# Row normalisation ahead of the transposes, copy evictions on ScalarE, and a later transpose of the residual, in a hybrid decoder layer on one core

## The chip, the cores and the metric

One NeuronCore of a Trainium2 chip runs the whole layer as one program. The metric is the device time of one execution in microseconds (us). Engine names: PE = TensorE matmul, PEld = TensorE weight load, DVE = VectorE, ACT = ScalarE, POOL = GpSimd, SP = SyncE, whose queue issues nearly all DMAs.

## The reference

Two groups of rows share one set of weights: 1024 prompt rows and 32 sample rows (8 sequences of 4), each of 1024 numbers.

```python
h = RMSNorm(x) * norm_mix_w
p = h @ w_in     # 5640 columns: q|k|v (512 each), conv q|k|v (1536), z (512), a, b (4+4), gate_A, gate_B (1024 each)
# branch A: stick-breaking attention, 8 heads x 64, strictly causal
s = sigmoid(q.k/8 + bias[head]);  w[i,j] = s[i,j] * prod_{j<l<i} (1 - s[i,l]);  o_A = w @ v
# branch B: conv of width 4, SiLU, l2norm, gated delta rule over chunks, 4 heads x 128, then norm and silu(z)
x = x + (sigmoid(gate_A) * (o_A @ w_pa) + sigmoid(gate_B) * (o_B @ w_pb)) @ w_o
x = x + relu(RMSNorm(x) @ w_up)^2 @ w_down;   y = RMSNorm(x)
```

The sample rows attend to 256 cached positions through a page table and have their own conv and delta states. All is float32. k, v, the last conv rows and the final states are outputs too.

## The kernel before

Everything is kept transposed: features on the 128 partitions, the 1056 rows (tokens) along the free dimension. A float32 product is made of three matmuls on parts rounded to fp32r: hi x hi, hi x lo, lo x hi (`dense`, L124 to L129), where ACT writes hi as a rounded copy and DVE writes lo = value - hi.

**Start (L76 to L238).** Nine row tiles `xn` are loaded; then the weights of the first two projections (`load_w`, L109) are queued on SP between the stores of `xT_d`. Each raw tile is transposed by PE (`xtp`, 8 transposes of 128x128), DVE multiplies by the norm weight (`xw`, L217), ACT keeps a raw copy `xs` (L218), which is stored to DRAM as `xT_d` for the residual, and `xw` is split into `xh`, `xl`, four column chunks `CX` of 256, 256, 256 and 288 tokens. Beside it `token_sum` and `finish_r` work out each row's 1/rms: a Square with sum on ACT (L192), a power on POOL (L105), a diagonal times ones on PE (`prb`, L201). The result R holds it for every token on all partitions. So the normalisation is not in `xh`, `xl`; every eviction of a projection multiplies by R on DVE.

**Projections (`proj`, L240).** A job is 128 columns of `w_in`: per chunk 24 matmuls into a PSUM bank, then an eviction. With the argument f set the banks are `psf` (two), else `psd` (two). Jobs: four heads of branch B, k, q, v, z each (`conv_job` L344, `z_job` L365); q, k, v of attention in pairs of heads (L753; tiles `ft`, three slots in pool `fk`); 16 gate jobs (`pd_g`, L978 to L990), whose result goes through a Sigmoid in place (L988) and to DRAM `gA_d`, `gB_d`.

**Attention (L886 to L975).** `attn_load` brings q and k of one head from DRAM onto both partition halves and splits them (L900 to L904). `weights` then works for each block of 128 queries: scores `sc` on PE, Sigmoid on ACT, mask and 1 - s on POOL (L917, L920), a backward product scan on DVE (L924), the product s x scan (L925), transposes `wt` on PE, copies on ACT, and `po` on PE, copied to `oT` by DVE (L954). Heads 0 to 5 go one after another, heads 6 and 7 together (`attn_last`).

**Order.** The source order is the priority. A planner runs through a modelled timeline and gives each engine the ready instruction of highest priority, so later jobs fill gaps of earlier ones: attention's q, k, v and the gates run inside branch B's chain and the cached attention, and the product with `w_pb` (`pb`, L1045 to L1056) runs beside attention. On the chip each engine then works through its list in that fixed order, SP's queue too. Memory is a stack: `xh`, `xl` and `fk` lie in pools closed by `xctx.close()` (L993), and the tiles of `pb` (`tb`, `obh`, `obl`) are laid over them; each waits until the tile under it is free.

After attention come `pa` with `w_pa` and the merge, `w_o` with the residual read from `xT_d` (L1159), and the channel mixer.

## Time and profile before

| | |
|---|---|
| runs shown | 1778.04, 1778.16, 1778.8 us; median 1778.16 |
| profiled execution | 1763.56 us, span 1761.9 us, clock 0.995 |
| instructions | 34413 |
| DMA | 224.91 MB, 39.4% of 16 engines on the main queue |

The span is the time from the first to the last recorded instruction. A row of "windows" gives, for a stretch of it, how long each engine was busy, in the order PE, PEld, DVE, ACT, POOL, with instruction counts, then the granted TensorE clock, the DMA share and GB/s. A row of "lines" groups the instructions of one source line: busy time and mean ns of one, then the idle time ahead of them with what ended it. In a timeline the first number is the start, the second the length, and brackets hold the idle time before.

### The profile page before, as it was taken

To read this page: it belongs to the slowest core of one execution; us is meant where nothing else is said; L and a number is where in the kernel's file an instruction comes from. 1 tells how busy PE (TensorE), PEld (TensorE's weight loads), DVE (VectorE), ACT (ScalarE), POOL (GpSimd) and SP (SyncE) were. 2 spreads that over 40 slices of the span, in tenths; PEclk is the share of its full clock that TensorE was granted. 3 is DMA by queue.
4 is the path that set the end of the run, shared out by engine and by line. 5 is a ranking of instruction groups with operands and counts; after the bars stand their busy time and mean duration, and the time that the engine had idled before them with its cause. 6 is when DMAs were issued, how large, how long until landed. Compare 5 with 4: busy or idle time off the path is not lost.

```text
span 1761.9 us, 34413 instructions
## 1 busy us (share of the span) xinstructions
PE 1703.9 (97%) x13831; PEld 1642.1 (93%) x13831; DVE 1236.8 (70%) x2584; ACT 746.0 (42%) x1370; POOL 229.1 (13%) x251
## 2 busy tenths in 40 slices
PE   7999999999999999999979999999999999999998
PEld 6999999999999778878869999999999899999998
DVE  6768587787436424899878576887777768788854
ACT  6441324232323122654533455554444564444354
POOL 1022111020001061465450000000000000000000
PEclk9999999999999999999999999999999999999999
DMA  7332132133426275354204645554443683532321
GB/s 223 76 103 78 43 103 85 57 116 90 135 79 186 81 237 146 106 164 110 75 35 129 183 129 151 158 150 147 136 152 131 232 293 129 171 121 95 123 73 76
DMA packets 229532, 224.91 MB, mean 128 GB/s; under 512 B 22186, under 2 KB 191507, under 8 KB 229372
## 3 DMA queue, kind: packets, MB, share of 16 engines
q1 hardware_dynamic: 225062, 214.09, 39.4%
q0 software_dynamic: 2560, 8.39, 1.5%
q8 instruction: 109, 1.79, 0.4%
q10 hardware_dynamic: 1750, 0.23, 0.1%
q14 instruction: 51, 0.42, 0.1%
HBM read 153.63 MB, written 69.04 MB: 126 GB/s over the span
## 4 chain that ended last, share of the span: by engine, by line
PE 78%; DVE 8%; issue 5%; DMA 5%; ACT 2%; POOL 1%; SPq 1%; POOLq 0%; ACTq 0%; DVEq 0%
PE pu L129 6%; PE pu L127 6%; PE pu L128 6%; PE pw L128 5%; PE pw L127 5%; PE pw L129 5%; PE pd_g L127 3%; PE pd_g L129 3%; PE pd_g L128 3%; DVE s L925 1%; DVE pr L924 1%; PE px L128 1%; PE pv L127 1%; PE px L129 1%; PE px L127 1%
## 5 line engine op out<-in xcount | busy, mean ns | idle before, releaser
L129 PE MATMUL pu<-Xh,ul 128*128 128x264 f32 x812 | 230.7, 285 | 0.0
L127 PE MATMUL pu<-Xh,uh 128*128 128x264 f32 x812 | 229.8, 283 | 0.4 <-ACT uh L1137 0.4
L128 PE MATMUL pu<-Xl,uh 128*128 128x264 f32 x812 | 230.1, 284 | 0.0
L127 PE MATMUL pw<-hc,w 128*128 128x264 f32 x728 | 206.2, 285 | 4.3 <-ACT w L1384 4.3
L128 PE MATMUL pw<-hc,w 128*128 128x264 f32 x728 | 206.9, 286 | 0.0
L129 PE MATMUL pw<-hc,w 128*128 128x264 f32 x728 | 202.2, 284 | 0.0
L127 PEld LDWEIGHTS pu<-Xh,uh 128*128 128x128 f32 x812 | 153.0, 188 | 0.7 <-ACT uh L1137 0.6
L128 PEld LDWEIGHTS pu<-Xl,uh 128*128 128x128 f32 x812 | 152.5, 188 | 0.0
L129 PEld LDWEIGHTS pu<-Xh,ul 128*128 128x128 f32 x812 | 152.0, 188 | 0.0
L127 PE MATMUL pd_g<-xh,wh_g 128*128 128x256 f32 (+1 forms) x512 | 150.0, 293 | 1.2 <-DVE gt L985 1.2
L129 PE MATMUL pd_g<-xh,wl_g 128*128 128x256 f32 (+1 forms) x512 | 149.6, 292 | 0.0
L128 PE MATMUL pd_g<-xl,wh_g 128*128 128x256 f32 (+1 forms) x512 | 149.1, 291 | 0.0
L127 PEld LDWEIGHTS pw<-hc,w 128*128 128x128 f32 x728 | 137.4, 189 | 4.5 <-ACT w L1384 4.5
L128 PEld LDWEIGHTS pw<-hc,w 128*128 128x128 f32 x728 | 137.2, 189 | 0.0
L129 PEld LDWEIGHTS pw<-hc,w 128*128 128x128 f32 x728 | 136.0, 189 | 0.0
L127 PEld LDWEIGHTS pd_g<-xh,wh_g 128*128 128x128 f32 x512 | 98.2, 192 | 5.3 <-issue 3.3
L128 PEld LDWEIGHTS pd_g<-xl,wh_g 128*128 128x128 f32 x512 | 98.2, 192 | 4.2 <-issue 4.1
L129 PEld LDWEIGHTS pd_g<-xh,wl_g 128*128 128x128 f32 x512 | 98.2, 192 | 2.7 <-issue 2.4
L924 DVE TENSOR_TENSOR_SCAN pr<-am 128x127 f32<-128x127 f32 (+7 forms) x64 | 91.2, 1432 | 5.7 <-POOL am L920 5.5
L105 POOL TENSOR_TENSOR fr<-fr,powc 128x3 f32<-128x3 f32 x4 | 3.4, 858 | 680.8 <-DVE fr L1495 645.1
L1384 ACT ACTIVATE w<-a 128x512 fp32r<-128x512 f32 x78 | 43.3, 621 | 94.0 <-PE pw L129 86.6
L129 PE MATMUL px<-mh,wl_wo 128*128 128x264 f32 x256 | 72.6, 287 | 1.3 <-DVE wl_wo L1138 1.2
(588 smaller groups left out, 5267.8 us busy)
## 6 DMA issues: line engine op xcount, KB each, us to landing
hc_d<-t SPq DMA_DIRECT2D x26, 924.0 KB, 4.9
hc<-hc_d SPq DMA_DIRECT2D x91, 264.0 KB, 3.0
a<-in_w_down_dram SPq DMA_DIRECT2D x52, 256.0 KB, 5.5
ws_g<-in_w_in_dram SPq DMA_DIRECT2D x16, 512.0 KB, 5.2
ws_wo<-in_w_o_dram SPq DMA_DIRECT2D x32, 256.0 KB, 3.0
ua<-in_w_up_dram SPq DMA_DIRECT2D x16, 512.0 KB, 4.9
ub<-in_w_up_dram SPq DMA_DIRECT2D x16, 512.0 KB, 4.2
gA_d<-gt SPq DMA_DIRECT2D x8, 528.0 KB, 3.6
```

The source lines that it names most:

```text
L105: G.tensor_tensor(out, in_, powc[: out.shape[0], which:which + 1].to_broadcast([out.shape[0], n]), op=ALU.pow)
L127: PE.matmul(pt[:, :n], lhsT=wh[k], rhs=xh[k], start=(k == 0), stop=False)
L128: PE.matmul(pt[:, :n], lhsT=wh[k], rhs=xl[k], start=False, stop=False)
L129: PE.matmul(pt[:, :n], lhsT=wl[k], rhs=xh[k], start=False, stop=(k == nk - 1))
L924: V.tensor_tensor_scan(pr[:, n - 2::-1], am_r, am_r, 1.0, op0=ALU.mult, op1=ALU.bypass)
L925: V.tensor_tensor(s[:, :n], s[:, :n], pr[:, :n], op=ALU.mult)
L1384: S_.activation(tl[:, 0], src, AF.Copy)
```

## The change

Several edits in one:

- Row tiles are normalised before they are transposed: Square on ACT, power on POOL, then one DVE instruction multiplies by 1/rms and by the norm weight, which is broadcast to all partitions as `nmb`. PE transposes the result; ACT writes `xh` and DVE `xl` straight from PSUM. R, `token_sum`, `finish_r` and `xw` are gone.
- The weights of the first three projections are loaded among the row tiles; `xn` has seven slots instead of nine.
- Projections of branch B and the gates are evicted by ACT, as Copy or, for the gates, as Sigmoid.
- q and k of attention are split at their eviction (hi by ACT, lo by DVE) and stored as two tensors each; `attn_load` only loads. `ft` has four slots.
- The scan loses its memset and is read one column shifted; `oT` is copied by ACT.
- After the gates a new loop loads the nine raw row tiles again, transposes them through the `psf` banks, copies them by ACT and stores `xT_d`, with two `ft` slots a tile.
- The last gate no longer lives in R, and goes through DRAM like the others.

```diff
-    nrow = sp.tile([8, P], F32, name="nrow", bufs=1)
-    SY.dma_start(nrow, norm_mix_w.rearrange("o (k p) -> (o k) p", p=P))
+    nmb = sp.tile([P, D], F32, name="nmb", bufs=1)
...
-    xns = []
+    winv = w_in[0].rearrange("(k p) n -> p k n", p=P)
+    xns, w0s = [], []
     for t in range(9):
-        xn = sp.tile([P, D], F32, tag="xn", name=f"xn{t}", bufs=9)
+        xn = sp.tile([P, D], F32, tag="xn", name=f"xn{t}", bufs=7)
         n = P if t < 8 else NS
         SY.dma_start(xn[:n], x_prompt[0, t * P:(t + 1) * P, :] if t < 8 else x_sample.rearrange("s t d -> (s t) d"))
         xns.append(xn)
+        if t == 1:
+            SY.dma_start(nmb, norm_mix_w.to_broadcast([P, D]))
+        if t in (1, 3, 5):
+            wp = wpool if t == 1 else gw if t == 5 else sp
+            st = wp.tile([P, 8, P], F32, tag="wst", name=f"ws_u0{t}", bufs=1)
+            col = {1: 2048, 3: 1536, 5: 2560}[t]
+            SY.dma_start(st, winv[:, :, col:col + P])
+            w0s.append(st)
...
@@ -183,52 +188,29 @@
         xhc[c] = xp.tile([P, KT, CX[c][1]], F32R, name=f"xh{c}")
         xlc[c] = xp.tile([P, KT, CX[c][1]], F32R, name=f"xl{c}")
     fk = pool("fk", stack=xctx)
-    winv = w_in[0].rearrange("(k p) n -> p k n", p=P)
     w0 = []
-
-    def token_sum(t):
-        n = P if t < 8 else NS
-        junk = sp.tile([P, D], F32, tag="junk", name=f"junk{t}", bufs=1)
-        S_.activation(junk[:n], xns[t][:n], AF.Square, accum_out=sst_[:n, t:t + 1])
-        V.tensor_scalar(sst_[:n, t:t + 1], sst_[:n, t:t + 1], 1.0 / D, EPS, op0=ALU.mult, op1=ALU.add)
-
-    def finish_r(t):
-        n = P if t < 8 else NS
-        rpow(rstd[:n, t:t + 1], sst_[:n, t:t + 1], 0, 1)
-        dg = sp.tile([P, P], F32, tag="dg", name=f"dg{t}")
-        V.tensor_scalar(dg[:n, :n], ident[:n, :n], rstd[:n, t:t + 1], None, op0=ALU.mult)
-        prb = gtile(f"prb{t}")
-        PE.matmul(prb[:, :n], lhsT=ones[:n, :], rhs=dg[:n, :n], start=True, stop=True)
-        V.tensor_copy(R[:, t * P:t * P + n], prb[:, :n])
-
     for t in range(9):
         n = P if t < 8 else NS
         c0 = t * P
         xn = xns[t]
-        xw = sp.tile([P, KT, P], F32, tag="xw", name=f"xw{t}")
-        xs = sp.tile([P, KT, P], F32, tag="xs", name=f"xs{t}")
+        junk = sp.tile([P, D], F32, tag="junk", name=f"junk{t}", bufs=1)
+        S_.activation(junk[:n], xn[:n], AF.Square, accum_out=sst_[:n, t:t + 1])
+        V.tensor_scalar(sst_[:n, t:t + 1], sst_[:n, t:t + 1], 1.0 / D, EPS, op0=ALU.mult, op1=ALU.add)
+        rpow(rstd[:n, t:t + 1], sst_[:n, t:t + 1], 0, 1)
+        V.scalar_tensor_tensor(xn[:n], xn[:n], rstd[:n, t:t + 1], nmb[:n], op0=ALU.mult, op1=ALU.mult)
+        cc = min(t // 2, 3)
+        co = c0 - CX[cc][0]
         for hf in range(2):
-            pt = ttile(f"xtp{t}_{hf}")
+            pt = (ttile, gtile)[hf](f"xtp{t}_{hf}")
             pv = pt.rearrange("p (k c) -> p k c", k=4)
             for k in range(4):
                 kk = hf * 4 + k
                 tr(pv[:, k, :n], xn[:n, kk * P:(kk + 1) * P], n)
-            ks = slice(hf * 4, hf * 4 + 4)
-            V.tensor_tensor(xw[:, ks, :n], pv[:, :, :n], nmw[:, ks].unsqueeze(2).to_broadcast([P, 4, n]), op=ALU.mult)
-            S_.activation(xs[:, ks, :n], pv[:, :, :n], AF.Copy)
-        cc = min(t // 2, 3)
-        co = c0 - CX[cc][0]
-        S_.activation(xhc[cc][:, :, co:co + n], xw[:, :, :n], AF.Copy)
-        V.tensor_tensor(xlc[cc][:, :, co:co + n], xw[:, :, :n], xhc[cc][:, :, co:co + n].bitcast(F32), op=ALU.subtract)
-        SY.dma_start(xT_d[:, :, c0:c0 + n].rearrange("k p c -> p k c"), xs[:, :, :n])
-        if t in (1, 2):
-            col = 2048 if t == 1 else 1536
-            w0.append(load_w(winv[:, :, col:col + P], f"u0{t}"))
-        if t % 2 == 1 or t == 8:
-            for u in range(t - t % 2, t + 1):
-                token_sum(u)
-            for u in range(t - t % 2, t + 1):
-                finish_r(u)
+            xh_ = xhc[cc][:, hf * 4:hf * 4 + 4, co:co + n]
+            S_.activation(xh_, pv[:, :, :n], AF.Copy)
+            V.tensor_tensor(xlc[cc][:, hf * 4:hf * 4 + 4, co:co + n], pv[:, :, :n], xh_.bitcast(F32), op=ALU.subtract)
+        if t in (1, 3, 5):
+            w0.append(load_w(None, f"u0{t}", gw if t == 5 else wpool, w0s[t // 2]))
...
@@ -348,12 +327,11 @@

         def evac(c, o, n, pt):
             if c < 3:
-                V.tensor_tensor(up[:, 3 + o:3 + o + n], pt[:, :n], R[:, o:o + n], op=ALU.mult)
+                S_.activation(up[:, 3 + o:3 + o + n], pt[:, :n], AF.Copy)
                 return
             m = NP - o
-            V.tensor_tensor(up[:, 3 + o:3 + NP], pt[:, :m], R[:, o:NP], op=ALU.mult)
-            V.tensor_tensor(us[:, i, :, 3:7], pt[:, m:n].rearrange("p (s t) -> p s t", s=8),
-                            R[:, NP:T].rearrange("p (s t) -> p s t", s=8), op=ALU.mult)
+            S_.activation(up[:, 3 + o:3 + NP], pt[:, :m], AF.Copy)
+            V.tensor_copy(us[:, i, :, 3:7], pt[:, m:n].rearrange("p (s t) -> p s t", s=8))
             V.tensor_scalar(cv, up[:, 0:NP], cwv(0, i), None, op0=ALU.mult)
             for j in range(1, 4):
...
@@ -366,7 +344,7 @@
         z = zp.tile([P, T], F32, tag="zz", name=f"z{h}")

         def evac(c, o, n, pt):
-            V.tensor_tensor(z[:, o:o + n], pt[:, :n], R[:, o:o + n], op=ALU.mult)
+            S_.activation(z[:, o:o + n], pt[:, :n], AF.Copy)
             if c == 3:
                 S_.activation(z, z, AF.Silu)
                 G.tensor_copy(zs[:, h, :], z[:, NP:T])
@@ -392,9 +370,9 @@
     def gdn_head(h):
         (jk, kT), (jq, qT), (jv, vT) = conv_job(4 + h, f"k{h}"), conv_job(h, f"q{h}"), conv_job(8 + h, f"v{h}")
         if h == 0:
-            proj([jk, jq], ws=w0)
+            proj([jk, jq], ws=w0[0:2])
             decays()
-            proj([jv], f=True, wp=gw)
+            proj([jv], f=True, ws=w0[2:3])
...
@@ -747,28 +725,46 @@
     vk = pool("vk", stack=bctx, side="right")


+    NFT = 4
     sbb = cst.tile([P, NH], F32, name="sbb")
     nc.scalar.dma_start(sbb, sb_bias.to_broadcast([P, NH]))
     for p in range(4):
         for nm, col, keep_s in (("q", 0, qsT), ("k", 512, ksT), ("v", 1024, vsT)):
-            f = fk.tile([P, T], F32, tag="ft", name=f"{nm}f{p}", bufs=3)
-
-            def ev(c, o, n, pt, f=f):
+            hi = lo = f = None
+            if nm != "q":
+                f = fk.tile([P, T], F32, tag="ft", name=f"{nm}f{p}", bufs=NFT)
+            if nm != "v":
+                hi = fk.tile([P, NP], F32R, tag="ft", name=f"{nm}h{p}", bufs=NFT)
+            if nm == "q":
+                lo = fk.tile([P, NP], F32, tag="ft", name=f"{nm}l{p}", bufs=NFT)
+
+            def ev(c, o, n, pt, f=f, hi=hi, lo=lo, keep_s=keep_s[:, p, :]):
+                m = min(n, NP - o)
                 with tc.high_priority():
-                    V.tensor_tensor(f[:, o:o + n], pt[:, :n], R[:, o:o + n], op=ALU.mult)
+                    if hi is not None:
+                        S_.activation(hi[:, o:o + m], pt[:, :m], AF.Copy)
+                    if lo is not None:
+                        V.tensor_tensor(lo[:, o:o + m], pt[:, :m], hi[:, o:o + m].bitcast(F32), op=ALU.subtract)
+                    if f is not None:
+                        S_.activation(f[:, o:o + m], pt[:, :m], AF.Copy)
+                    if m < n:
+                        V.tensor_copy(keep_s, pt[:, m:n])

             proj([(col + p * P, f"a{nm}{p}", ev)], f=True)
-            G.tensor_copy(keep_s[:, p, :], f[:, NP:T])
-            if nm != "v":
-                SY.dma_start((q_d if nm == "q" else k_d)[p], f[:, 0:NP])
             if nm != "q":
-                nt = fk.tile([P, NP], F32, tag="ft", name=f"nt{nm}{p}", bufs=3)
+                nt = fk.tile([P, NP], F32, tag="ft", name=f"nt{nm}{p}", bufs=NFT)
                 for hf, pt in enumerate(tr8(f, f"n{nm}{p}", lambda n_: dtile(n_, True))):
                     S_.activation(nt[:, hf * 512:(hf + 1) * 512], pt, AF.Copy)
                 dst = nk_prompt if nm == "k" else nv_prompt
                 SY.dma_start(dst[0, 0, :, :, 2 * p:2 * p + 2, :].rearrange("c t h d -> t c (h d)"), c8(nt))
                 if nm == "v":
                     SY.dma_start(v_d[p], c8(nt))
+            if nm == "k":
+                lo = f[:, 0:NP]
+                V.tensor_tensor(lo, lo, hi.bitcast(F32), op=ALU.subtract)
+            if nm != "v":
+                for dst, src in zip(q_d if nm == "q" else k_d, (hi.bitcast(F32), lo)):
+                    SY.dma_start(dst[p], src)


...
@@ -890,18 +886,11 @@
         kh = ak.tile([P, NP], F32R, tag="kh", name=f"kh{hh}")
         kl = ak.tile([P, NP], F32R, tag="kl", name=f"kl{hh}")

-        def load2(src, name):
-            t_ = ak.tile([P, NP], F32, tag="qd", name=f"{name}{hh}", bufs=1)
-            for r in range(2):
-                SY.dma_start(t_[64 * r:64 * r + 64], src[p, rs])
-            return t_
-
-        qd = load2(q_d, "qd")
-        S_.activation(qs, qd, AF.Copy)
-        V.tensor_tensor(qs[64:128], qd[64:128], qs[64:128].bitcast(F32), op=ALU.subtract)
-        kd_ = load2(k_d, "kd")
-        S_.activation(kh, kd_, AF.Copy)
-        V.tensor_tensor(kl, kd_, kh.bitcast(F32), op=ALU.subtract)
+        for r in range(2):
+            hs = slice(64 * r, 64 * r + 64)
+            SY.dma_start(qs[hs].bitcast(F32), q_d[r][p, rs])
+            SY.dma_start(kh[hs].bitcast(F32), k_d[0][p, rs])
+            SY.dma_start(kl[hs].bitcast(F32), k_d[1][p, rs])
         return qs, kh, kl

...
@@ -918,11 +907,11 @@
                         channel_multiplier=1)
         am = ak.tile([P, NP], F32, tag="am", name=f"am{hh}_{i}", bufs=2)
         G.tensor_scalar(am[:, :n], s[:, :n], -1.0, 1.0, op0=ALU.mult, op1=ALU.add)
+
         pr = ak.tile([P, NP], F32, tag="pr", name=f"pr{hh}_{i}")
-        V.memset(pr[:, n - 1:n], 1.0)
         am_r = am[:, n - 1:0:-1]
-        V.tensor_tensor_scan(pr[:, n - 2::-1], am_r, am_r, 1.0, op0=ALU.mult, op1=ALU.bypass)
-        V.tensor_tensor(s[:, :n], s[:, :n], pr[:, :n], op=ALU.mult)
+        V.tensor_tensor_scan(pr[:, n - 1:0:-1], am_r, am_r, 1.0, op0=ALU.mult, op1=ALU.bypass)
+        V.tensor_tensor(s[:, :n - 1], s[:, :n - 1], pr[:, 1:n], op=ALU.mult)
         wt = ak.tile([P, NP], F32, tag="wt", name=f"wt{hh}_{i}", bufs=2)
...
@@ -951,7 +940,7 @@
                         continue
                     PE.matmul(po[64 * r:64 * r + 64, 0:P], lhsT=vn[:, b, rs], rhs=wts[r][:, b * P:(b + 1) * P],
                               start=(b == 0), stop=(b == 2 * m + r))
-            V.tensor_copy(oT[:, m, :], po[:, 0:P])
+            S_.activation(oT[:, m, :], po[:, 0:P], AF.Copy)
         for r in range(2):
             SY.dma_start(o_d[p, rs, 0:NP].rearrange("d (m r c) -> d r m c", r=2, c=P)[:, r], oT[64 * r:64 * r + 64])
...
@@ -977,17 +966,26 @@

     for j in range(KT):
         for b, gd in ((0, gA_d), (1, gB_d)):
-            last = j == KT - 1 and b == 1
-            gt = R if last else fk.tile([P, T], F32, tag="ft", name=f"gt{b}_{j}", bufs=3)
+            gt = fk.tile([P, T], F32, tag="ft", name=f"gt{b}_{j}", bufs=NFT)

             def ev(c, o, n, pt, gt=gt):
                 with tc.high_priority():
-                    V.tensor_tensor(gt[:, o:o + n], pt[:, :n], R[:, o:o + n], op=ALU.mult)
+                    S_.activation(gt[:, o:o + n], pt[:, :n], AF.Sigmoid)

             proj([(3592 + b * D + j * P, f"g{b}_{j}", ev)], f=True)
-            S_.activation(gt, gt, AF.Sigmoid)
-            if not last:
-                SY.dma_start(gd[j], gt)
+            SY.dma_start(gd[j], gt)
+    for t in range(9):
+        n = P if t < 8 else NS
+        xn = fk.tile([P, D], F32, tag="ft", name=f"xr{t}", bufs=NFT)
+        SY.dma_start(xn[:n], x_prompt[0, t * P:(t + 1) * P, :] if t < 8 else x_sample.rearrange("s t d -> (s t) d"))
+        xs = fk.tile([P, KT, P], F32, tag="ft", name=f"xs{t}", bufs=NFT)
+        for hf in range(2):
+            pv = dtile(f"xrp{t}_{hf}", True).rearrange("p (k c) -> p k c", k=4)
+            for k in range(4):
+                kk = hf * 4 + k
+                tr(pv[:, k, :n], xn[:n, kk * P:(kk + 1) * P], n)
+            S_.activation(xs[:, hf * 4:hf * 4 + 4, :n], pv[:, :, :n], AF.Copy)
+        SY.dma_start(xT_d[:, :, t * P:t * P + n].rearrange("k p c -> p k c"), xs[:, :, :n])
     ofb0 = zp.tile([P, 4, 256], F32, tag="zz", name="ofb0")
...
@@ -1045,14 +1043,14 @@
         for jj in range(2):
             j = 2 * jp + jj
             tb = tbs[j]
-            if jp and j < KT - 1:
+            if jp:
                 with tc.issue_after(mark.ins), tc.issue_after(wq[0].ins):
                     SY.dma_start(tb, gB_d[j])
             for c, (o, n) in enumerate(CX):
                 pt = dtile(f"pb{j}_{c}", f=True)
                 dense4(pt, wb, jj, [obh[c][:, k] for k in range(4)], [obl[c][:, k] for k in range(4)], n)
                 with tc.high_priority():
-                    V.tensor_tensor(tb[:, o:o + n], pt[:, :n], (tb if j < KT - 1 else R)[:, o:o + n], op=ALU.mult)
+                    V.tensor_tensor(tb[:, o:o + n], pt[:, :n], tb[:, o:o + n], op=ALU.mult)
```

## Rows read from the trace of the kernel before

**Rows 1.** Page, part 1: busy us of each engine, share of the span, instructions.

```profile
PE 1703.9 (97%) x13831; PEld 1642.1 (93%) x13831; DVE 1236.8 (70%) x2584; ACT 746.0 (42%) x1370; POOL 229.1 (13%) x251
```

**Rows 2.** Windows: stretch and length, then busy us of each engine (instructions), clock.

```profile
0.00:22.00 22.00, 11.93 (x47) 9.46 (x47) 12.41 (x40) 15.98 (x27) 6.09 (x17) 1.00 0.88 291
...
53.00:60.00 7.00, 5.65 (x45) 5.44 (x44) 6.95 (x12) 2.62 (x3) 1.46 (x2) 1.00 0.43 106
60.00:600.00 540.00, 535.40 (x4551) 529.03 (x4549) 362.76 (x918) 170.62 (x324) 67.86 (x67) 1.00 0.32 94
...
700.00:740.00 40.00, 37.91 (x296) 33.04 (x294) 34.10 (x56) 22.24 (x40) 17.34 (x24) 1.00 0.32 88
740.00:868.00 128.00, 119.91 (x979) 103.21 (x979) 118.29 (x187) 68.76 (x137) 67.57 (x74) 1.00 0.42 122
868.00:917.00 49.00, 38.46 (x280) 28.66 (x279) 43.04 (x55) 26.61 (x56) 31.97 (x27) 0.97 0.16 50
917.00:1762.00 845.00, 827.46 (x6692) 822.98 (x6690) 609.90 (x1220) 399.00 (x725) 6.13 (x6) 1.00 0.45 146
```

**Rows 3.** Timeline of PE, first 40 us: start, length, instruction, count.

```profile
5.01 1.97 PE L102 MATMUL xtp<-ident,xn 128*128 128x128 f32 x8 [2.14 <-DMA xn<-in_x_prompt_dram]
...
21.97 0.58 PE L127 MATMUL pd_uk<-xh,wh_u 128*128 128x256 f32 x1
...
27.69 0.60 PE L102 MATMUL xtp<-ident,xn 128*128 128x128 f32 x4
28.05 0.36 PE L128 MATMUL pd_uk<-xl,wh_u 128*128 128x256 f32 x1
...
30.27 0.28 PE L128 MATMUL pd_uk<-xl,wh_u 128*128 128x256 f32 x1
30.39 0.28 PE L129 MATMUL pd_uk<-xh,wl_u 128*128 128x256 f32 x1
```

**Rows 4.** Timeline of SP's queue, first 40 us: DMA issues.

```profile
1.27 8.88 SPq L91 DMA_DIRECT2D xn<-in_x_prompt_dram  x8
...
12.12 1.30 SPq L113 DMA_DIRECT2D ws_u<-in_w_in_dram  x1
```

**Rows 5.** Timeline of ACT, first 40 us.

```profile
20.86 1.06 ACT L117 ACTIVATE wh_u<-ws_u 128x1024 fp32r<-128x1024 f32 x1
```

**Rows 6.** Timeline of POOL, first 40 us.

```profile
7.86 0.56 POOL L105 TENSOR_TENSOR rstd<-sst__142,powc 128x1 f32<-128x1 f32 x1 [4.67 <-DVE sst__142 L193]
```

**Rows 7.** Lines of DVE by shape, whole span: busy us, mean ns, idle before.

```profile
L359 DVE SCALAR_TENSOR_TENSOR cvk<-upk,vec,cvk 128x1024 f32<-128x1024 f32 x12 | 15.2, 1269 | 0.0
```

**Rows 8.** Lines of ACT by shape, whole span.

```profile
L1442 ACT ACTIVATE acc<-pw 128x264 f32<-128x264 f32 x32 | 11.5, 389 | 12.9 <-PE pw L129 12.1 <-DMA hc_d<-t 0.7
...
L218 ACT ACTIVATE xs<-xtp 128x512 f32<-128x512 f32 x16 | 9.4, 594 | 11.5 <-issue 7.7 <-DVE xw L217 2.5 <-PE prb L201 1.3
```

**Rows 9.** Lines of DVE by shape, 700 to 868 us.

```profile
L901 DVE TENSOR_TENSOR qs<-qd,qs 64x1024 fp32r<-64x1024 f32 x7 | 9.7, 1381 | 4.1 <-ACT qs L900 3.9
L904 DVE TENSOR_TENSOR kl<-kd,kh 128x1024 fp32r<-128x1024 f32 x7 | 8.9, 1278 | 1.5 <-ACT kh L903 1.5
...
L954 DVE COPY oT<-po 128x128 f32<-128x128 f32 x23 | 6.4, 278 | 3.9 <-PE po L952 3.9
```

**Rows 10.** Windows of PE for tile pb alone.

```profile
740.00:868.00 128.00, 56.04 (x383) 1.00 0.42 122
```

**Rows 11.** Timeline of ACT, 440 to 625 us.

```profile
563.13 1.28 ACT L988 ACT_TABLE_LOAD   x1
...
565.53 1.28 ACT L660 ACT_TABLE_LOAD   x1
```

**Rows 12.** DMA issues, whole span: count, KB each, median us to landing.

```profile
xn<-in_x_prompt_dram SPq DMA_DIRECT2D x8, 512.0 KB, 6.5
xT_d<-xs SPq DMA_DIRECT2D x8, 512.0 KB, 3.7
...
cgb<-cg_d SPq DMA_DIRECT2D x4, 512.0 KB, 6.2
```

More of the change, by code (lines that the diff above doesn't have):

```diff
@@ L76, in hybrid_step @@
     uc = pool("uc", stack=gctx, side="right")
+    gw = pool("gw", stack=gctx, side="right")
     sctx = ExitStack()
     sp = pool("sp", 2, stack=sctx, side="right")
-    nrow = sp.tile([8, P], F32, name="nrow", bufs=1)
-    SY.dma_start(nrow, norm_mix_w.rearrange("o (k p) -> (o k) p", p=P))
+    nmb = sp.tile([P, D], F32, name="nmb", bufs=1)
     vrow = sp.tile([P, P], F32, name="vrow", bufs=1)
@@ L107, in hybrid_step, with load_w @@
     wq = [None]
-    def load_w(src, name, wp=wpool):
-        st = wp.tile([P, 8, P], F32, tag="wst", name=f"ws_{name}", bufs=1)
-        nk, ncol = src.shape[1], src.shape[2]
-        stv = st if nk == 8 else st.rearrange("p a b -> p (a b)").rearrange("p (k c) -> p k c", k=nk)
-        wq[0] = SY.dma_start(stv, src)
+    def load_w(src, name, wp=wpool, st=None):
+        nk = 8 if st is not None else src.shape[1]
+        if st is None:
+            st = wp.tile([P, 8, P], F32, tag="wst", name=f"ws_{name}", bufs=1)
+            stv = st if nk == 8 else st.rearrange("p a b -> p (a b)").rearrange("p (k c) -> p k c", k=nk)
+            wq[0] = SY.dma_start(stv, src)
         hi = wp.tile([P, 8, P], F32R, tag="wh", name=f"wh_{name}")
@@ L138, in hybrid_step @@
     z_d = dr.tile([GH, P, NP], F32, name="z_d")
-    q_d = dr.tile([4, P, NP], F32, name="q_d")
-    k_d = dr.tile([4, P, NP], F32, name="k_d")
+    q_d = [dr.tile([4, P, NP], F32, name=f"q{x}_d") for x in "hl"]
+    k_d = [dr.tile([4, P, NP], F32, name=f"k{x}_d") for x in "hl"]
     v_d = dr.tile([4, P, NC, P], F32, name="v_d")
@@ L144, in hybrid_step @@
     tv_d = dr.tile([GH, 4, NC, 32, 32], F32, name="tv_d")
-    nps = gtile("nps")
-    tr(nps[:, :8], nrow, 8)
-    nmw = cst.tile([P, 8], F32, name="nmw")
-    V.tensor_copy(nmw, nps[:, :8])
     vps = gtile("vps")
@@ L160, in hybrid_step @@
     gnw = vec[:, 64:65]
-    R = keep.tile([P, T], F32, name="R")
     rstd = cst.tile([P, 9], F32, name="rstd")
@@ L248, in proj @@
                 evac(c, o, n, pt)
-    gw = pool("gw", stack=gctx, side="right")
     gk = pool("gk", stack=gctx, side="right")
@@ L308, in decays @@
             ab2 = gk.tile([8, 384], F32, tag="x2", name=f"ab2{c}")
-            V.tensor_tensor(ab2[:, :n], pt[32:40, :n], R[32:40, o:o + n], op=ALU.mult)
+            V.tensor_copy(ab2[:, :n], pt[32:40, :n])
             m = min(n, NP - o)
-            V.tensor_tensor(abT[:, o:o + m], pt[0:8, :m], R[0:8, o:o + m], op=ALU.mult)
-            V.tensor_tensor(abT[:, o:o + m], abT[:, o:o + m], ab2[:, :m], op=ALU.add)
+            V.tensor_tensor(abT[:, o:o + m], pt[0:8, :m], ab2[:, :m], op=ALU.add)
             if m < n:
-                V.tensor_tensor(abT2, pt[0:8, m:n], R[0:8, NP:T], op=ALU.mult)
-                V.tensor_tensor(abT2, abT2, ab2[:, m:n], op=ALU.add)
+                V.tensor_tensor(abT2, pt[0:8, m:n], ab2[:, m:n], op=ALU.add)
         pabt = gtile("pabt")
```

## The prediction

> **What bounds the kernel now.** The page's first part comes first: PE is busy 1703.9 of 1761.9 us [rows 1], so 58 us of PE idling is all that can be won without taking work off it. Then the windows, to see where the 58 lie [rows 2]. Length minus PE busy: 22 - 11.93 = 10.1 us at the start; 1.4 from 53 to 60; 4.6 from 60 to 600; from 700 to 917, the attention, 2.1 + 8.1 + 10.5 = 20.7; after 917, in 845 us, 17.5. Between 60 and 600 the gates and the attention projections fill every gap of branch B, so a faster engine there buys nothing. Attention is the place where another engine sets the pace: DVE is busy 118.29 of 128 us from 740 to 868 and 43.04 of 49 after. The rest are short waits.
>
> So the time after is the time before, plus the PE work added, plus the change of PE's idling. Four terms.
>
> **A, the start: -7.5 us (bounds -10 and -3).** The first projection starts at 21.97 [rows 3]. Its weights are issued at 12.12, behind all row tiles and a store [rows 4], and split only at 20.86 [rows 5]. After the change they are the fourth transfer; eight issues took 8.88 us [rows 4], so the fourth goes out near 4.5 us. The first transpose now starts at 5.01 [rows 3], which is when tile 0 is there; two tiles and the weights more put the last of these four near 9.
>
> New is a chain ahead of each transpose. Tile 0: Square 1.06 (an ACT pass over 1024 columns, as the weight copy [rows 5]), power 0.56 [rows 6], the product with two factors 1.27 [rows 7], but not before `nmb` has landed near 7.5: transposable at 8.7. Eight transposes take 1.97 at this stage [rows 3], ACT's copy of the last half 0.59 [rows 8], DVE's subtraction half of 1.28 [rows 9]: split at 12. Tile 1 follows about 1.5 later, when DVE and PE come free. Its first four k are split earlier, so PE begins at about 13, 9 us sooner. By 22 the kernel before has transposed five tiles, the new one only two by 13; three are paid later, at 0.36 for four transposes (27.69 to 28.05 [rows 3]), 2.2 us. The `prb` products and the copies of R go (about -1): -9 + 2.2 - 1 = -7.8. The 1.4 us from 53 to 60, where `wl_uv` was late, can go too, as these weights now come early. What is late next is DVE: nine tiles at 1.27 + 1.28 and three weight splits are 27 us from 7.5 on, the last tile ready near 35. PE, at 0.12 a matmul (30.27 to 30.39 [rows 3]), needs it near 37. That margin is thin, so I take -7.5. If `nmb` lands as late as another load that spreads one row over all partitions, 6.2 [rows 12], the start is at 15 to 16: hence -3 with some queueing. -10 is the chain with no queueing and the 1.4 won.
>
> **B, attention: -11.5 us (bounds -20 and +12).** From 700 to 868 DVE loses `qs` 9.7, `kl` 8.9 and the `oT` copies 6.4 [rows 9], 25 us of the 34.1 + 118.3 that it is busy [rows 2]; the memsets and gate evictions there are worth less. On ACT the two split copies of a head go and short ones come, and ACT has 69 of 128 busy. Attention then could run one sixth faster, if PE lets it. Of PE's 119.91 us from 740 to 868, 56.04 are `pb` [rows 10], so attention's own is 64, in a stretch that DVE alone would bring down to about 106: 60 per cent of PE, the other 40 per cent wants a filler. `pb` is 56 us of filler, enough to reach into 868 to 917, which has none now; that is where the 20.7 can go.
>
> But `pb` lies behind the new loop. The pools of `xh`, `xl` (67.6 KB a partition) and `fk` close together; `tb` and its neighbours take 46.5 KB, then `obh3`, `obl3`, `obh0`, `obl0` to 63.9, and `obh1` reaches into the first `ft` slot. So until the loop frees its slots only chunk 0 of `pb` runs, and with two weight buffers only for four j: 4 x 12 x 0.12 = 5.8 us. The loop itself gives PE 7. How long it lasts, L: a load 6.5, eight transposes 0.72, two copies 1.2, a store 3.7 [rows 3, 8, 12] are 12.1 us for a tile; four slots keep two tiles in flight, so 9 x 12.1 / 2 = 54, a little less as a load can go out while the copies run: 50. Idling is then 0.4 x 50 - 7 - 5.8 = 7.2, and 2.1 before 740 as now: 9.3 in place of 20.7. The bounds: all but about 1 us of it goes, or L is the serial 109 us.
>
> **C, PE work added: +7 us (6.5 to 11).** 18 groups of four transposes, 0.36 each, or 0.60 if each pays its full length [rows 3]. Nothing hides this where PE is full; where it idles, the idle above is already counted with it. ACT's 18 copies of 0.59 lie in a half-idle engine.
>
> **D, evictions on ACT: +1 us (0 to +5).** An ACT eviction of 264 columns takes 0.39 [rows 8]; a chunk of 24 matmuls takes 2.9 and there are two banks, so an eviction may be 2.9 late before PE stops. ACT is in order, and what stands ahead of it is short but for one place: the functions of the cached delta step fall among the gates. There a Sigmoid set is loaded at 563.13 for 1.28 and the Exp set at 565.53 [rows 11]. With a gate eviction due every 2.9 us, Exp work of about 1.7 between two loads holds it 4.3: 1.4 beyond the banks, about once. Zero if the planner keeps them apart, 5 if it happens three times.
>
> The Trainium skill (ScalarE: Activation LUTs, "What ACT_TABLE_LOAD costs") prices a change of function set at 1283 ns of loading and 1380 ns of draining, and advises batching by set, which speaks against spreading 16 Sigmoids into 64. The trace agrees on the 1283, but the 2.40 us between the two loads of [rows 11] are filled by 1.28 and one Sigmoid pass of 1056 columns (near 1.1, by the 1.06 of [rows 5]), so a drain has no room there. By the Trainium skill's 2.66 that one hold would be 7 us and D about +4.
>
> Hidden: the second copies of q and k in DRAM and half again as many loads per head (six for four) are covered by the two buffers of each head's operands; uncovered, each costs one landing, about 4 us, at a head's start. At q and k, ACT makes two copies in 2.9 us of PE, which it can.
>
> **Sum.** -7.5 - 11.5 + 7 + 1 = -11 us: 1763.6 to 1752.6 in a profiled execution. The runs shown lie 14.6 above the profiled one; I move the median by the same amount: 1778.2 - 11 = 1767.
>
> **Rivals.**
> *The fillers fit fully.* The loop falls into gaps, L is 30 or less, PE is full until the end of attention: idling 2, B = -18.7, and the granted clock, 0.97 from 868 to 917 [rows 2], stays at 1, worth 1.5. With D at 0: -7.5 - 20.2 + 7 = -20.7, so 1757. For it: PE idles in attention only where `pb` has run out. Against: `pb` now comes later than before.
> *DVE was not the bound, or its relief is given back.* B = 0: -7.5 + 7 + 1 = +0.5, so 1779. For it: the product of s and the scan follows POOL and ACT in a chain that only six buffers of s hide. Against: DVE at 92 per cent from 740 to 868.
> *The new loop locks attention's filler out (slower).* SP is in order: if each store, waiting for ACT, stands ahead of the next load, the tiles go one at a time, L = 109, idling 0.4 x 109 - 7 - 5.8 + 2.1 = 32.9, B = +12.2, and the sum is +12.7: 1791. It turns slower from L about 86 on. For it: loads and stores of one loop share the queue with attention's loads. Against: the slots are four, and the planner sees the stores.
>
> **How the numbers follow.** Forecast 0.45, full fit 0.22, no relief 0.18, lock-out 0.15. The forecast's own range, with A and D at their bounds, is 1760 to 1774. A run of this kernel can tell 0.2 per cent, 3.6 us, from no change, so faster is below 1774.6: nearly all of the first two and a third of the third, 0.72; slower 0.16; same 0.12. The range 1750 to 1786 leaves out the best of the second case and most of the fourth.
>
> **What would show it.** First `pd_uk` near 13 us; idling under 12 us from the loop to attention's end, with `pb` running past it; the loop's nine tiles within 60 us; DVE below 85 per cent there; no PE wait on an ACT eviction above 2 us. I am wrong if `pb` starts its second chunk more than 86 us after the last gate, if the first projection begins after 18, or if PE waits often for ACT between 60 and 600.

## The result, and the profile after

The changed kernel is not faster but a little slower: 1782.03 us (median of 20 runs) where the kernel before had 1777.62 (20 runs), ratio 1.0022, 95% interval 1.0012 to 1.0032. Two repeats gave 1.0010 (0.9997 to 1.0024) and 1.0011 (0.9999 to 1.0023). Forecast was 1767, 11 us faster.

The kernel before took about 1778 us in some sessions and about 1763 in others, so every number below is a ratio to the kernel before in the same session. The rows of before have a span of 1761.9 us; I read the changed kernel from its second repeat, span 1761.1 (the profiled execution of the first comparison has 1773.2).

The page's engine line, to be held against [rows 1]:

```profile
PE 1704.7 (97%) x13884; PEld 1645.5 (93%) x13884; DVE 1156.3 (66%) x2312; ACT 785.8 (45%) x1563; POOL 200.2 (11%) x239
```

DVE lost 80 us and PE's line is nearly the same: 56.4 us of idling for 58.0. Where it lies, in the windows of the changed kernel (columns as in [rows 2], the same stretches):

```profile
0.00:22.00 22.00, 10.46 (x44) 9.12 (x45) 13.34 (x29) 14.93 (x25) 5.58 (x16) 1.00 0.93 308
53.00:60.00 7.00, 6.61 (x56) 6.30 (x55) 6.97 (x9) 3.00 (x3) 0.42 (x1) 1.00 0.40 104
60.00:600.00 540.00, 531.11 (x4457) 518.29 (x4457) 322.02 (x804) 209.35 (x469) 59.79 (x55) 1.00 0.34 101
700.00:740.00 40.00, 40.00 (x342) 36.39 (x341) 25.43 (x26) 21.31 (x48) 11.99 (x22) 1.00 0.46 134
740.00:868.00 128.00, 116.54 (x888) 94.73 (x887) 102.64 (x112) 81.43 (x184) 68.57 (x84) 0.96 0.68 181
868.00:917.00 49.00, 46.28 (x398) 43.53 (x397) 23.48 (x38) 11.00 (x20) 3.09 (x2) 1.00 0.30 96
917.00:1761.00 844.00, 826.26 (x6669) 822.51 (x6667) 613.45 (x1219) 399.09 (x722) 6.12 (x6) 0.99 0.45 146
```

Read length minus the first number. From 868 to 917 the idling fell from 10.5 to 2.7 us, as forecast. From 740 to 868 it rose from 8.1 to 11.5, with DVE at 80 per cent instead of 92, and PE issued 888 instructions for 979 at a granted clock of 0.96. From 60 to 600 it rose from 4.6 to 8.9. In those two stretches the gain went.

What fills attention, by tile (first and last start us stand after the durations), changed kernel: `xrp` is the new loop over raw rows.

```profile
L137 PE MATMUL pd_g<-xh,wh_g x512: 274/282/402, 466.2 to 751.6; 128*128 128x256 f32 x128, 128*128 128x288 f32 x43
...
L111 PE MATMUL xrp<-ident,xr x72: 221/272/421, 754.8 to 814.3; 128*128 128x128 f32 x64, 32*128 32x32 f32 x8
...
L137 PE MATMUL pb<-obh,wh_pb x128: 274/283/562, 819.2 to 915.5; 128*128 128x256 f32 x96, 128*128 128x288 f32 x32
...
L941 PE MATMUL po<-wt,vn x432: 272/273/476, 675.7 to 833.1; 128*64 128x128 f32 x144
L956 PE MATMUL po<-wt,vn x144: 272/273/323, 834.7 to 889.3; 128*64 128x128 f32 x144
```

The same tiles of the kernel before, run beside it:

```profile
L127 PE MATMUL pb<-obh,wh_pb x128: 275/283/401, 735.5 to 863.4; 128*128 128x256 f32 x96, 128*128 128x288 f32 x32
...
L952 PE MATMUL po<-wt,vn x432: 272/273/324, 698.8 to 869.5; 128*64 128x128 f32 x144
L967 PE MATMUL po<-wt,vn x144: 272/273/476, 870.7 to 918.2; 128*64 128x128 f32 x144
```

Attention (`po`) begins 23 us earlier and ends 29 us earlier, but it is nearly as long as before, 214 us for 219. Between the last gate and the first `pb` lie 68 us in which PE has nothing beside attention but 72 transposes, and `pb` ends 52 us later than before, now behind attention.

### The profile page after: what moved, and what is told of

Read it like the earlier page. It is cut to its first block, busy times and chain, and to the rows that moved or that the text cites. A ratio compares the mean times of both kernels' runs of the same rounds, so it can differ in the third digit from the quotient of the medians.

```text
span 1773.2 us, 34494 instructions
## 1 busy us (share of the span) xinstructions
PE 1710.3 (96%) x13884; PEld 1646.6 (93%) x13884; DVE 1156.5 (65%) x2312; ACT 785.3 (44%) x1563; POOL 205.0 (12%) x239
## 4 chain that ended last, share of the span: by engine, by line
PE 70%; issue 12%; POOL 6%; DVE 6%; DMA 4%; ACT 1%; SPq 0%; POOLq 0%; DVEq 0%; ACTq 0%; another core or an unknown queue 0%
PE pu L139 6%; PE pu L137 6%; PE pu L138 6%; PE pw L138 5%; PE pw L137 5%; PE pw L139 5%; POOL am L909 3%; POOL s L906 2%; PE px L138 1%; PE px L139 1%; PE pv L137 1%; PE px L137 1%; PE pv L139 1%; PE pv L138 1%; PE pd_g L137 1%
```

## The experiments

Ratios are to the kernel before in the same session; 0.001 is 1.8 us.

**No late loop, or only its loads and copies.** Theory one was that the raw loop is the loss, by PE work and by keeping `pb` out; theory two, that the evictions moved to ACT are. First without the loop. This version leaves out the raw residual: normalised rows are stored in its place.

```diff
-    for t in range(9):            # load, 8 transposes, 2 copies, store
-...
+    for c, (o, n) in enumerate(CX):
+        SY.dma_start(xT_d[:, :, o:o + n]..., xhc[c].bitcast(F32))
```

> The changed kernel without the late loop over raw rows: no row loads, no 72 raw transposes, no copies; the residual reads the normalised rows instead, stored from xh in four transfers, so the output is not the reference's. Theory 'the raw loop is the loss' (its PE work, and pb kept out until it ends): 9.2 us of PE busy time go, and with pb following the gates directly most of the idling of 768 to 832 (5.0 us) and of 832 to 972 (some 10 us) goes too: 15 to 20 us under the changed kernel's 1782, so 1762 to 1767. Theory 'the evictions on ACT are the loss': only the PE work goes, 1773, and the idling before 460 us stays.

0.9877 (0.9860 to 0.9894). Run again beside the changed kernel:

> The changed kernel without raw tiles (normalised rows stored for the residual, not the reference's), for a difference to the changed kernel on one chip. From last gate to first px the changed kernel took 206.4 us, this one 189.5 on the other chip: theory 'the raw loop costs 17' says 16 to 18 us between the two on any chip, 10 of it PE work and place each in about equal parts by the runs with untransposed copies and with raw tiles at the start. Theory 'it costs 25', as the two ratios to before suggest: 24 to 26.

0.9894 (0.9878 to 0.9910): 1743.29 us, and the changed kernel, its second repeat, 1764.49 in that session. So the loop costs 21 us, between the two guesses, and without it the rest of the change gains 19 to 22. Then the loop without the transposes of its eight wide tiles, `xs` copied from `xn`. This version leaves out a correct residual, which reads untransposed rows:

> The changed kernel with its late loop over raw rows, but the eight wide tiles are copied without being transposed (the residual then reads untransposed rows, so the output is not the reference's): loads, copies and stores as before, 64 of 72 transposes gone. Theory 'the loop loses by its place: pb waits for its tiles': most of the 25 us stay, 6 to 8 us under the changed kernel. Theory 'it loses by PE work': 15 us or more under it, near the kernel without raw tiles.

0.9962 (0.9948 to 0.9976), with the changed kernel at 1.0010 beside it: 8.6 us for 64 transposes, 9.7 for 72. That is the most that their PE work can be, since the loop also gets shorter: from the last gate to the first `pb` it is 44 us (769.1 to 812.9) and 67 in its partner (769.5 to 836.5). PE's busy time differs by 6.3 us (1710.6 and 1704.2), 7.1 for 72. So 11 to 14 us of the 21 are not PE work.

**The changed kernel twice more, and the kernel before once**, with no edit, to tell sessions from kernels:

> The changed kernel itself, run beside the others. The chip of the last runs gives the kernel before 1763.5 us, the one of the first comparison 1777.6, so the two profiles compared so far may come from unlike chips. If the ratio 1.0022 holds, 1767. Theory 'the loss sits in the cached attention, 600 to 660' (359 matmuls there in the changed kernel's profile, 511 in that without raw tiles, whose PE order is the same up to the loop): this profile shows 360 again. Theory 'that was the other chip': about 510, last dav at 648 and last gate near 750, and the whole loss of 25 us against the kernel without raw tiles lies after 740.

> The kernel before, for a profile on the same chip as the next three. Runs so far came from two chips, told apart by the time of the kernel before: near 1763.5 and near 1778. The changed kernel's last gate is at 769.5 us on the second; the kernel without raw tiles, whose PE order up to the loop is the same, has it at 750.5 on the first. Theory 'the slower chip loses its 15 us in the cached attention, in every kernel': where before runs at 1778 its last gate is near 752, where it runs at 1763 at 736, as in the profile shown. Theory 'only the changed kernel loses there': 736 on both.

> The changed kernel beside the kernel before. On a chip where before has 1778: ratio 1.001 to 1.002 again. On one where it has 1763: theory 'every kernel loses the same there' says 1.001 to 1.002 there too; theory 'only the changed kernel does' says its last gate comes at 750, and 0.995 to 0.998, faster.

The first repeat has 1.0010 and its last gate at 769.5; the second has 1.0011 and 751.6, where the kernel before beside it (1.0006 to itself, 0.9994 to 1.0017) has 732.3. So the ratio is the same in both sessions, though the changed kernel's own trace shifts by 18 us.

**The same loop elsewhere.** One raw tile ahead of each pair of gate jobs:

```diff
+    raw_tile(8)
     for j in range(KT):
+        raw_tile(j)
```

> The changed kernel with each raw row tile loaded, transposed and stored ahead of one pair of gate jobs, and not in a loop behind them. The PE work is the same; pb is no longer kept out after the last gate. Theory 'the raw loop is the loss by keeping pb out': 6 to 11 us under the changed kernel, 1771 to 1776. Theory 'only its PE work counts' and theory 'the evictions on ACT are the loss': 1781 to 1783, unchanged.

1.0008 (0.9992 to 1.0024): no better. The tiles share four slots and one queue with the gates; from 464 to 540 PE idles 4.6 us, where the changed kernel idles 0.3, and the last gate comes at 788.5.

At the start, each raw tile transposed, copied and stored ahead of its normalised one (twice), and then with the normalised tile in a tile of its own, so that raw ones rank behind it:

```diff
+        xm = sp.tile([P, D], F32, tag="xm", bufs=2)
-        V.scalar_tensor_tensor(xn[:n], xn[:n], rstd..., nmb[:n], ...)
+        V.scalar_tensor_tensor(xm[:n], xn[:n], rstd..., nmb[:n], ...)
+        # behind the transposes of xm: those of xn, copies to xs, store
```

> The changed kernel with the raw tiles transposed, copied and stored at the start, each ahead of its normalised tile, and the late loop gone. PE work is that of the changed kernel (144 transposes), and pb follows the gates. Theory 'place': the start idles on PE anyway, so this is within 8 us of the kernel without raw tiles: 1742 to 1750 where before has 1763.5. Theory 'PE work': 1755 or more. If ACT's 18 further copies delay the first projection, that shows in the start itself (first pd_uk after 18 us).

0.9944 (0.9926 to 0.9962).

> The version with each raw tile ahead of its normalised one, again: its 0.9944 came from a session in which the kernel before took 1779; here it is compared at whatever level this chip has. 0.993 to 0.996 if the ratio does not depend on that level; 0.998 or more if its gain came only from the stretch that was slow there.

0.9936 (0.9916 to 0.9956): the same ratio in another session.

> The changed kernel without the late loop; raw tiles are transposed at the start, but rank behind the normalised tile (which gets a tile of its own), so that they fall into PE's waiting there. PE work is that of the changed kernel. Theory 'place': 0.990 to 0.995 of before; first pd_uk near 16, as the raw copies no longer stand ahead of xh on ACT (20.5 where each raw tile came first). Theory 'PE work, wherever it is': 0.998 to 1.002.

0.9931 (0.9909 to 0.9952), 1752.4 us: the fastest version that computes everything, and it beats both kernels. All 144 transposes are in it. Its tiles, and the first of its PE timeline:

```profile
L111 PE MATMUL xrp<-ident,xn x72: 221/273/476, 5.2 to 41.6; 128*128 128x128 f32 x64, 32*128 32x32 f32 x8
...
L137 PE MATMUL pb<-obh,wh_pb x128: 274/283/401, 769.4 to 896.9; 128*128 128x256 f32 x96, 128*128 128x288 f32 x32
...
L965 PE MATMUL po<-wt,vn x144: 272/273/323, 845.7 to 896.7; 128*64 128x128 f32 x144
```

```profile
5.19 1.94 PE L111 MATMUL xrp<-ident,xn 128*128 128x128 f32 x8 [5.19 <-DMA xn<-in_x_prompt_dram]
...
18.00 0.37 PE L137 MATMUL pd_uk<-xh,wh_u 128*128 128x256 f32 x1
18.20 0.28 PE L138 MATMUL pd_uk<-xl,wh_u 128*128 128x256 f32 x1
18.32 0.28 PE L139 MATMUL pd_uk<-xh,wl_u 128*128 128x256 f32 x1
```

`pb` and attention end together, at 897: that is the balance which the changed kernel misses by 26 us (915.5 and 889.3) and the kernel before by 55 the other way (863.4 and 918.2). By 60 us this kernel has done 227 projection matmuls, the changed one 240; so 72 transposes more have cost 1.5 us by then, at 0.12 each. That is not their whole price: the last `pd_av` (attention's last projection) comes at 468.5, in the changed kernel at 463.1, and against the versions without raw tiles (0.9894 and 0.9877) the whole kernel is 6.5 to 9.5 us slower. Against the changed kernel, with the same PE work, it is 14 us faster: that is what the place is worth.

**Is it the slots?** The forecast let `pb` wait for the loop's slots. So the loop got a pool of its own, in half tiles, at its place and then behind `pb` in the source:

```diff
+    rk = pool("rk", stack=actx, side="right")
-        xn = fk.tile([P, D], F32, tag="ft", ...)
+        xn = rk.tile([P, 512], F32, tag="xr", ..., bufs=2)
+        xs = rk.tile([P, 4, P], F32, tag="xs", ..., bufs=1)
```

> The changed kernel with the raw loop at its place in the source, but in half tiles of 512 columns in a pool of its own beside attention's tiles, so that xh, xl and the ft slots are free when the gates end. PE work, copies and bytes are the same, loads and stores twice as many of half the size. Theory 'lock-out': pb starts within 8 us of the last gate, pb no longer runs 10 us or more past attention's end, and 8 to 12 us go against the changed kernel: ratio 0.994 to 0.997. Theory 'the loop's loads, stores and copies disturb attention': the same loss stays, 1.000 to 1.002.

1.0042 (1.0027 to 1.0057), slower. The tiles show why:

```profile
L111 PE MATMUL xrp<-ident,xr x72: 221/272/330, 739.4 to 849.9; 128*128 128x128 f32 x64, 32*128 32x32 f32 x8
...
L137 PE MATMUL pb<-obh,wh_pb x128: 274/283/400, 852.5 to 921.4; 128*128 128x256 f32 x96, 128*128 128x288 f32 x32
...
L1025 ACT ACTIVATE obh<-ofb x1: 1047/1047/1047, 743.8 to 743.8; 128x1024 fp32r<-128x1024 f32 x1
L1026 DVE TENSOR_TENSOR obl<-ofb,obh x1: 1310/1310/1310, 746.6 to 746.6; 128x1024 fp32r<-128x1024 f32 x1
```

With one `xs` buffer the loop is serial, 110 us, and `pb` starts behind its last transpose although no slot is shared any more and the operands of its first chunk, `obh` and `obl`, are ready at 748. What is still shared are the two `psf` banks: both take them by `dtile(..., True)`, in the order of the source. So my test took one lock away and left the other.

> As the one with the pool of its own, but the loop stands behind pb in the source, so that it ranks below pb. Theory 'lock-out': pb runs as in the kernel without raw tiles, and the transposes fall where PE idles near attention's end, or are paid in full: 10 to 14 us under the changed kernel, 0.993 to 0.996, so not worse than the one ahead of pb. Theory 'disturbs attention': 1.000 to 1.002.

1.0121 (1.0103 to 1.0139). `pb` is free now (751 to 883) and the next user of `psf`, `pa`, is locked instead. From 905 to 930 PE has 48 instructions in 25 us, at a granted clock of 0.67 (1.00 up to 910, 0.50, the lower of the two levels, from 915):

```profile
905.00:930.00 25.00, 8.94 (x48) 6.24 (x44) 3.06 (x5) 6.87 (x12) 0.00 (x0) 0.67 0.71 209
```

**The attention edits alone**, on the kernel before (raw tiles stay at the start, R stays):

> The kernel before with the attention edits alone: q and k split at the projection and stored as two parts, no split in attn_load, no memset ahead of the scan, oT copied by ACT. Raw rows are still transposed at the start. Theory 'DVE was the bound of attention, and the raw loop took the gain': attention ends 15 us or more earlier with pb beside it, 8 to 12 us under the kernel before: 1766 to 1770. Theory 'the relief is worth nothing, since PE is full with pb or waits for other engines there': 1776 to 1779.

0.9985 (0.9972 to 0.9997), 2.6 us. DVE's busy time from 740 to 868 falls from 118 to 102 us and PE's stays at 120; `pb` ends at 861.0 and attention at 915.8, about as before.

**The evictions.** Conv inputs, z, k and v whole and the gates evicted by DVE again, with the late loop, without it, and with the loop behind `pb`:

```diff
-                S_.activation(up[:, 3 + o:3 + o + n], pt[:, :n], AF.Copy)
+                V.tensor_copy(up[:, 3 + o:3 + o + n], pt[:, :n])
-                    S_.activation(gt[:, o:o + n], pt[:, :n], AF.Sigmoid)
+                    V.tensor_copy(gt[:, o:o + n], pt[:, :n])
+            S_.activation(gt, gt, AF.Sigmoid)
```

> The changed kernel with the plain evictions of the projections back on DVE: conv inputs, z, the whole copy of k and v, and the gates (copied by DVE, then one Sigmoid pass for each tile as in the kernel before). The rounded copy of q and k stays on ACT. Theory 'the evictions on ACT are the loss': the 5 us that the start gains are still there at 460 us, the clock from 600 to 680 is over 0.9 again: 6 to 10 us under the changed kernel, 1772 to 1776. Theory 'the raw loop is the loss': within 2 us of the changed kernel's 1782, or slower, since DVE gets back 60 us of work.

1.0000 (0.9989 to 1.0011).

> The changed kernel without raw tiles (normalised rows stored for the residual, not the reference's), with the plain evictions on DVE. Against the one without raw tiles and evictions on ACT (0.9877 and 0.9894): theory 'evictions on ACT cost 3 us or more before 464 us': 0.985 to 0.987. Theory 'no cost': 0.988 to 0.990.

0.9969 (0.9952 to 0.9986): without the loop, 13 to 16 us slower than with ACT. Theory two falls: with the loop the evictions on ACT make next to no difference (1.0000 against 1.0010 and 1.0011), without it they are a gain. With DVE the last gate comes 7 us earlier (739.2 for 746.5), but the cached attention ends 20 us later (its last product `dav` at 663.8 for 643.8), and prompt attention runs on to 912 where `pb` ends at 878. ACT's copies leave DVE to the cached attention.

> The last one with the plain evictions of the projections on DVE too, as in x3. By the traces x3 was 3 us ahead of the changed kernel at 464 us. Theory 'evictions on ACT cost PE time that nothing gives back': 2 to 5 us under the last one, 0.990 to 0.994 of before. Theory 'DVE is needed in attention, and there the gates' evictions are in the way': equal or slower.

1.0072 (1.0056 to 1.0088), 9 us under its partner with ACT, but both are spoilt by the lock on `pa`.

**One transpose for both.** Rows times 1/rms are transposed, weighted after it, and the residual is recovered by a product with the rms, on POOL:

> A version that computes everything with one transpose for each tile: rows times 1/rms are transposed, the norm weight goes on after it, an unweighted copy is stored as xT_d, and ahead of the residual POOL multiplies it by the rms, spread over the partitions by nine products with ones. No late loop. If PE work and the place of the loop are both what it costs, it comes near the kernel without raw tiles, 1743 to 1750 where before has 1763.5; the start is 1 to 3 us later than the changed kernel's, as ACT and DVE have one more pass over each tile.

0.9992 (0.9977 to 1.0008): no gain. The first projection starts at 21.3 instead of 15.4, and `px`, the product with `w_o`, takes 112 us for 101. There DVE is full, and then POOL works too; PE waits for DVE for 4.7 of the 11 us:

```profile
1050.00:1060.00 10.00, 8.39 (x69) 8.17 (x68) 10.00 (x19) 4.08 (x8) 0.00 (x0) 1.00 0.47 145
1060.00:1070.00 10.00, 8.96 (x70) 8.34 (x68) 8.79 (x16) 6.68 (x12) 3.73 (x1) 1.00 0.32 94
```

> The version that recovers the residual, mended: its row of rms goes through DRAM and is spread by one load, without products with ones, and DVE multiplies in place of POOL. In the first form the nine products stood in a row at 976 to 985 with PE idle 2.5 us, and px lost some 6 us more around 1050 to 1080, where POOL and DVE worked at once: 11 us over the 101 of the other kernels from first to last px. Mended: px takes 101 to 103, and the whole is 8 to 10 us under the first form's ratio of 0.9992, so 0.994 to 0.995. If DVE's 16 further products delay the residual: 0.997 or more.

1.0080 (1.0063 to 1.0097): worse still. The row of rms is now stored in 4-byte pieces; from 20 to 40 us the DMA share is 1.05 at 135 GB/s, where the first form moved 214 GB/s at 0.73. `px` takes 117 us, and PE waits for DVE for 6.3 us of it. How much each of the two costs is not shown. In both versions `pb` and attention end within 1 us of each other (918.5 and 917.9; 906.7 and 906.2), so that balance alone does not make a kernel fast.

## Why the prediction was wrong

**Where 13 us went.** Forecast -11, measured +2 in the repeats. The loop costs 21, where the forecast had 14: C's 7 and, in B, 7.3 for idling 9.3 instead of 2. The rest of the change gains 19 to 22, where the forecast had 25: A's 7.5, B's 18.7 for a full fit, less 1 for D. One sum is off beside that: with A and D at their bounds the forecast's own range is 1764 to 1776, not 1760 to 1774.

**B failed, in the step "until the loop frees its slots only chunk 0 of `pb` runs".** None of it ran: `pb` starts at 819.2, behind the last raw transpose. Two locks held it; the forecast had the first only for the later chunks, and the second not at all. First, chunk 0 was not free either: its operand `obh` is written only at 817.4, after the loop's last copy, and `obl` at 821.1, for which PE waits 2.1 us, though the load of their source was issued at 540:

```profile
L1024 ACT ACTIVATE obh<-ofb x1: 1087/1087/1087, 817.4 to 817.4; 128x1024 fp32r<-128x1024 f32 x1
```

With the loop in a pool of its own it is written at 743.8, so my count of which slots lie under which tile did not hold; why chunk 0 waited for the whole pool is not shown. Second, the two banks: that run shows that they keep `pb` back even when its operands are ready. The loop took 60 us (754.8 to 814.3), where I had 50, and its place cost 11 to 14 us, not 7. The third rival, lock-out, named the right effect, but by another cause (tiles that go one at a time) and with a turning point of 86 us; here 68 us from the last gate to `pb` were enough to take the gain. The length does matter: 110 us made it 1.0042.

**B failed too in "attention then could run one sixth faster".** DVE at 92 per cent was no bound: with 16 us less work on it, attention alone gained 2.6 us, and attention still took 214 us, although from 754 to 819 neither DVE (51 of 65 us) nor PE (59) was full. What DVE won it spends waiting for POOL's `am` (1 - s). From 700 to 890 us, in the kernel before (us in total, times, longest):

```profile
DVE pr L924 <- POOL am L920: 4.5, 8, 1.1
```

and in the changed kernel:

```profile
DVE pr L913 <- POOL am L909: 30.4, 26, 2.6
```

POOL in turn waits 80.9 us for ACT's Sigmoid there, which works on PE's scores. That is the chain that the second rival, "DVE was not the bound", names. Its +0.5 us is also nearest to the measured +2, but that part is luck: it has neither the loop's 21 us nor the gain of 19 to 22, which happen to cancel.

What the change gives attention is an earlier start, 23 us, since the cached attention ahead of it gets DVE sooner (last `dav` 648.1 for 665.7). This I had not seen. It goes with the evictions: back on DVE, without the loop, they bring the last `dav` to 663.8 and take 13 to 16 of the 19 to 22 us.

**A was about half: 240 projection matmuls by 60 us for 213, 27 x 0.12 = 3.2 us**, inside the bounds. The first starts at 15.4, not 13: a table load of 1.28 stands ahead of the first Square, and the first transpose waits for DVE until 10.17. Idling in the first 22 us is no less. And until 22.1 us the matmuls are 0.21 apart, then 0.12. The windows' granted clock is 1.00 for both, but in the run with the attention edits alone the same product is 0.21 apart from 23.4 to 27.2 us, where the granted clock is 0.50 from 22 to 26; so I read the 0.21 as the lower of the two levels, 1.2 GHz:

```profile
15.43 0.58 PE L137 MATMUL pd_uk<-xh,wh_u 128*128 128x256 f32 x1 [0.79 <-ACT xh L210]
...
21.88 0.41 PE L139 MATMUL pd_uq<-xh,wl_u 128*128 128x256 f32 x1
22.09 0.38 PE L137 MATMUL pd_uq<-xh,wh_u 128*128 128x256 f32 x1
22.30 0.28 PE L138 MATMUL pd_uq<-xl,wh_u 128*128 128x256 f32 x1
22.43 0.28 PE L139 MATMUL pd_uq<-xh,wl_u 128*128 128x256 f32 x1
```

I took 0.12 from rows at 30 us for a stretch in which PE had just begun to work.

**C was right in mechanism and about right in size:** 7.1 us by PE's busy time, 9.7 at most, for 7. At the start the same transposes cost 6.5 to 9.5 us in all.

**D was right for the gates and missed the attention projections.** A gate eviction holds PE once, for 1.1 us. Among the gates, table loads stand at 543.60, 545.44, 551.90 and 554.96; the work between the first two ends at 545.41, 0.03 ahead of the second. The trace thus agrees with the 1283 ns of a load in the Trainium skill (ScalarE: Activation LUTs, "What ACT_TABLE_LOAD costs"), and shows no room for its 1380 ns of draining. But "at q and k, ACT makes two copies in 2.9 us of PE, which it can" did not hold. PE's waits from 60 to 464 us, changed kernel (us in total, times, longest):

```profile
PE pd_aq L137 <- DVE ql L747: 2.5, 1, 2.5
PE pd_uv L137 <- ACT upv L330: 1.1, 1, 1.1
PE t_nk L111 <- ACT ntk L757: 1.1, 2, 0.9
PE s L528 <- ACT ntv L757: 0.9, 1, 0.9
PE l L484 <- DVE U L475: 0.9, 1, 0.9
```

For q, ACT's copy and DVE's subtraction follow each other on one bank. Idling from 60 to 464 is 7.3 us, in the kernel before 3.1, and the last `pd_av` is at 463.1 for 460.2: the start's gain is used up there.

**What would show it.** "Idling under 12" and "`pb` running past attention" came half true (14.2 from 700 to 917; it ran past), "nine tiles within 60 us" true at the edge, "DVE below 85 per cent" true and worth little, "first `pd_uk` near 13" wrong by 2.4. None of the three signs of being wrong came: the first projection began at 15.4, the second chunk of `pb` 76 us after the last gate (827.5), and PE waits for ACT six times between 60 and 600 us, 4.4 us in all. They did not cover the step that failed.

What stays open: how much of the 11 to 14 us of place is `pb` locked out and how much the loop's loads and copies beside attention (DMA share 0.93 from 754 to 819), since no version had the loop there without either lock.

## What to carry to other kernels

Before a job is put ahead of a filler, list everything the two hand to each other in source order, PSUM banks as well as SBUF slots and queues: one shared ring is enough to lock the filler out for as long as the job lasts. On a kernel that is full on PE, look for the stretch where PE waits anyway and put the added work there: the same 72 transposes cost the whole kernel 6.5 to 9.5 us at the start and 21 us in the middle of attention. And a busy engine at 92 per cent is a bound only if what waits for it is the end of the chain: look for what it will wait for when it gets less work. Ask too whether filler and chain end together, but that alone decides nothing: two versions here that end so gain nothing.
